# One decoder step on one core: page gathers spread over the first stage, window copies in the last stage, and the first RWKV inversion split with dense products between its parts

## The chip, the cores and the metric

The kernel runs on 1 core of one Trainium2 chip. The metric is the device time of one execution in microseconds (us). The engines of the core are PE (TensorE, with its weight loads shown apart as PEld), DVE (VectorE), ACT (ScalarE), POOL (GpSimd) and SP (SyncE, which here only issues DMAs).

## The reference, cut to what matters

One layer of a hybrid decoder, for a prompt of 512 tokens and for 8 samples of 4 tokens each with a paged cache:

```
x <- x + 1/2 * SwiGLU_1(RMSNorm(x))            # first stage
z  = RMSNorm(x) @ W_in                         # one projection, columns split among the groups
     NSA group:  compressed, selected and window attention branches over paged caches
     RWKV group: token shift, decay, delta-rule state (64 x 64 per head), group norm
x <- x + concat(NSA_out, RWKV_out) @ W_out
x <- x + 1/2 * SwiGLU_2(RMSNorm(x))            # last stage
y  = RMSNorm_final(x)

def cmp_rows(pool, new, pe, w1, w2):           # the samples' compressed keys and values
    past = pool[page_table].reshape(n, PAST_LEN, N_KV_NSA, HEAD_DIM)
    return ... compress(past, pe, w1, w2) ...
def compress(rows, pe, w1, w2):
    blk = rows.reshape(n, length // CMP_BLOCK, CMP_BLOCK, N_KV_NSA, HEAD_DIM) + pe[:, None, :]
    return gelu(einsum('nbcgd,cde->nbge', blk, w1)) @ w2
wb = cache_win_k.shape[1]                      # the window caches, moved on by four rows, are outputs
kw_all = concatenate([cache_win_k, kw], axis=1);  ...  kw_all[:, -wb:], vw_all[:, -wb:]
```

D_MODEL is 1024, D_FF 2816, and all data are fp32. The 8 samples have 16 pages each, 128 pages in all, whose keys and values the first SwiGLU stage gathers and compresses beside its own work.

## The kernel before

The token axis (544 columns: 512 prompt and 32 sample tokens) stays as two halves of 272 columns (HW), and the model axis lies on the partitions. An fp32 product is made of three matmuls on split operands: high part by high part, low by high, high by low (`dense`, L156; `hh`, `hl` are the split activations, `ah`, `al` those of the hidden layer, `wh`, `wl` the split weights). So one 128x128 weight block costs six matmuls of 272 columns.

`wload` (L141) brings a weight tile in chunks of four blocks: SP issues the DMA into `wraw` (L148), ACT copies to `wh` (L150), DVE subtracts to `wl` (L152). Each of the three has three buffers. A chunk feeds 24 matmuls on PE.

`ffn` (L161) is both SwiGLU stages. It runs over 22 hidden tiles `f`, with a gate and an up tile of two chunks each, into PSUM tiles `acc`, and then over 8 output tiles of 22 blocks each. That is 3168 matmuls of 272 columns a stage. In the first stage it calls a hook, `block_step` (L921), before each of the 44 weight tiles of the first part. The hook brings small tables in (f = 1, f = 3), computes the gather indices `idx` (f = 3), issues the copies of the window caches from DRAM to DRAM (f = 14 to 21: two of 254 KB for each f, on SP), and at the steps in `CSTEP` calls `block_pages` (L947).

`block_pages` works on the 128 pages in five groups of 25 or 26 (`CG`). One call multiplies the group that lies in the tile `cp` by the compression weights (64 small matmuls into `hid`, L956), and then gathers the next group into `cp` (`gather`, L915: one indirect DMA on POOL's queue for each page, 128 KB, L918). `cp` has one buffer, so a group's gathers wait for the matmuls of the group before, and then all go out one behind the other.

After the first stage `mix` (L351) does the norm, the input projection (`win_tile`: 48 dense matmuls for each tile) and the RWKV group. `rwkv_prep` (L528) runs twice (`si` 0 and 1), over two head pairs each time, numbered p = 0 to 3 here: it shifts five projected tiles, computes decay and keys, and builds for each chunk of 32 tokens a triangular matrix `L`, with the products of `ar` and `bk` (L598), transposes (L607, L614) and sums (L497, L562, L563). `rwkv_inverse` (L632) inverts all of them for one `si`: DVE transposes `L` into `ivA` (L636, L638), then solves the diagonal 16x16 blocks in a loop of 15 steps of a product and a sum (L653, L654), and transposes the result into `ivDt` and `ivDn` (L656, L658). PE then assembles the off-diagonal blocks in four groups of small matmuls (L664; L672 and L674; L685; L693) with copies on ACT, DVE and POOL between. `rwkv_chain` runs the recurrence.

A scheduler orders the instructions on each engine from their dependences and the order in which the program issues them; those that are passed to `keep_in_program_order` (as `mm` does for a matmul) stay in the order of the program among themselves. In the part around the first inversion the scheduler places the dense matmuls of later projection tiles where PE would wait. Then follow the NSA branches, attention, the output projection and the second `ffn`, which has no hook.

Of the kernel before, what the change touches and what calls it, by code (L numbers as in the profile page):

```python
# [17 lines left out]
KT = 8  # L18
# [8 lines left out]
CSTEP = (8, 15, 22, 29, 36, 43)  # L27
# [21 lines left out]
class Step:  # L49
# [91 lines left out]
    def wload(self, src, n):  # L141
        nc = self.nc
        out = []
        src = src.rearrange("p (k f) -> p k f", f=128)
        for k0 in range(0, n, WK):
            m = min(WK, n - k0)
            w = self.wp.tile([128, WK, 128], F32, name="wraw", tag="wraw", bufs=WB[0])
            nc.sync.dma_start(w[:, :m], src[:, k0:k0 + m])  # L148
            wh = self.wp.tile([128, WK, 128], F32R, name="wh", tag="wh", bufs=WB[1])
            nc.scalar.activation(wh[:, :m], w[:, :m], AF.Copy)  # L150
            wl = self.wp.tile([128, WK, 128], F32R, name="wl", tag="wl", bufs=WB[2])
            nc.vector.tensor_sub(wl[:, :m], w[:, :m], wh[:, :m].bitcast(F32))  # L152
            out += [(wh[:, j], wl[:, j]) for j in range(m)]
        return out
# [184 lines left out]
    def run(self):  # L339
        I, O = self.I, self.O  # L340
        self.setup()
        self.early_w = None
        with ExitStack() as st:
            self.cpool = self.pool("cmp", 1, st)
            self.first_norm()
            self.ffn(I["wg1"], I["wu1"], I["wd1"], I["x"], self.x1, V_MX, self.block_step)
        self.mix()
        self.ffn(I["wg2"], I["wu2"], I["wd2"], self.x2, None, None)
        self.sA.close()

    def mix(self):  # L351
        nc = self.nc
        r = self.norm_end()
        with ExitStack() as st:
# [4 lines left out]
            with ExitStack() as s0:  # L359
                un0 = self.pool("u0", 1, s0, side="right")  # L360
                with ExitStack() as s2:
                    self.rwkv_setup(s2)
                    self.lanes = "p"
                    S0 = self.rwkv_prep(0, r, un0)
                    self.lanes = "q"
                    self.rwkv_inverse(S0[0])
                    self.lanes = "p"
                    S1 = self.rwkv_prep(1, r, un1)
# [4 lines left out]
                self.rwkv_inverse(S1[0])  # L373
# [103 lines left out]

    def shifted(self, i, col, r, tp, xs):
        nc = self.nc
        p = self.win_tile(i)  # L480
# [47 lines left out]
    def rwkv_prep(self, si, r, up):  # L528
# [101 lines left out]
        return L, BK, UV, ar, pcp  # L630

    def rwkv_inverse(self, L):  # L632
        nc, un = self.nc, self.un
        A = un.tile([128, 32, 32], F32, name="ivA", tag="iA")
        Lt = L.rearrange("p x c t -> p t (x c)")
        nc.vector.transpose(A, Lt[:, 0:32])  # L636
        for s in (slice(32, 64), slice(96, 128)):
            nc.vector.transpose(A[s], Lt[s, 32:64])  # L638
# [19 lines left out]
        nc.vector.transpose(Dn.rearrange("p b t -> p t b"), N)  # L658
        grp = [(hh, q, 64 * hh + 32 * q) for q in range(2) for hh in range(2)]
        T = un.tile([128, 16, 16], F32, name="ivT", tag="iN")  # L660
        p = self.ps()
        for c in range(16):
            for hh, q, g in grp:
                nc.tensor.matmul(p[g:g + 32, c * 16:c * 16 + 16], L[g:g + 16, hh, c, 32 * q:32 * q + 32], Dt[g:g + 16, 16 * hh + c, 0:16],  # L664
                                 start=True, stop=True)
        nc.scalar.activation(T, p[:, 0:256].rearrange("p (c s) -> p c s", s=16), AF.Copy, scale=self.half)
# [3 lines left out]
        for c in range(16):  # L670
            for hh, q, g in grp[0:2]:
                nc.tensor.matmul(pt[g:g + 32, c * 16:c * 16 + 16], Dn[g:g + 32, 16 * hh + c], T[g:g + 32, c], start=True, stop=True)  # L672
            for hh, q, g in grp:
                nc.tensor.matmul(pz[g:g + 16, c * 16:c * 16 + 16], T[g:g + 32, c], Dn[g:g + 32, 16 * hh + c, 16:32], start=True, stop=True)  # L674
# [7 lines left out]
        for c in range(16):  # L682
            for hh in range(2):
                g = 64 * hh
                nc.tensor.matmul(p[g + 32:g + 64, c * 32:c * 32 + 32], L[g:g + 32, hh, c, 32:64], Dt[g:g + 32, 16 * hh + c], start=True, stop=True)  # L685
# [4 lines left out]
        for c in range(16):  # L690
            for hh in range(2):
                g = 64 * hh
                nc.tensor.matmul(p[g:g + 32, c * 32:c * 32 + 32], W[g + 32:g + 64, c], L[g + 32:g + 64, hh, c, 32:64], start=True, stop=True)  # L693
        for hh in range(2):
            s = slice(64 * hh, 64 * hh + 32)
            nc.scalar.activation(L[s, hh, :, 32:64], p[s].rearrange("p (c t) -> p c t", t=32), AF.Copy)

# [223 lines left out]
    def block_step(self, step):  # L921
        nc, I, O = self.nc, self.I, self.O
        c = self.cpool
        if step in CSTEP:
            self.block_pages(CSTEP.index(step))
# [3 lines left out]
        if f > 13:  # L929
            n = f - 14  # L930
            for o, x in ((O["owk"][n, :, 0:508], I["wkT"][n, :, 4:512]), (O["owv"][n, 0:508], I["wv"][n, 4:512])):
                self.tc.keep_in_program_order(nc.sync.dma_start(o, x))
        if f == 1:
            self.table_loads()
        if f == 3:
# [9 lines left out]
            nc.vector.tensor_scalar(self.idx, pf[:, 0:128], 128.0, pf[:, 128:129], op0=OP.mult, op1=OP.add)  # L945

    def block_pages(self, at):  # L947
        nc, I, c = self.nc, self.I, self.cpool
        if at > 0:
            i = at - 1  # L950
            k0, m = CG[i], CG[i + 1] - CG[i]
            w = 4 * m + (4 if i == 0 else 0)
            ph = self.ps()
            for j in range(32):
                for x in range(2):
                    nc.tensor.matmul(ph[64 * x:64 * x + 64, 0:w], self.w1[:, x, j], self.cp[:, 0:w // 4, x, j], start=j == 0, stop=j == 31)  # L956
# [675 lines left out]
```

## Time and profile before

| What | Value |
|---|---|
| Runs, us | median 1522.66 of 3, 1521.82 to 1527.6 |
| The profiled execution, us | 1521.93 |
| Its span, us | 1520.1 |
| Mean granted clock of PE | 0.929 of full |
| PE busy | 1367.9 us, 90% of the span, 13337 matmuls |
| DVE, ACT, POOL busy, us | 707.0, 512.1, 250.7 |
| Traffic | 163.25 MB by DMA, mean 107 GB/s |
| Chain that ended last | PE 80%, of which the dense line L159 63%; issue 7%; DVE 6%; ACT 3% |

The profiled execution's own time stands 1.83 us above its span. The page gives shares of the whole span; the stages differ, and they are looked at one by one below. Stretches are named by the time from the span's start: the norm at the first stage's end is at 569.5 us, the RWKV group follows, the output projection starts at 1059.4 us and the last stage right behind it. In a row of a timeline the bracket at the end tells how long the engine was idle before it and what released it; "issue" means that the profile shows nothing that it waited for.

### The profile page before, as it was taken

How to read it: one execution, taken by the hardware profiler on the slowest of the kernel's cores; microseconds unless marked ns; L12 is line 12 of the kernel's file. 1: busy time of each engine (PE TensorE's matmuls, PEld its weight loads, DVE VectorE, ACT ScalarE, POOL GpSimd, SP SyncE). 2: the span in 40 equal slices, each digit the busy share in tenths (PEclk: the TensorE clock that was granted, in tenths of full speed). 3: DMA queues.
4: the chain of work that ended last, by engine and by line, in shares of the span. 5: the costliest groups of instructions: out<-in, count | busy, mean ns of one | idle time of the engine just before them, and what ended most of it. 6: DMA issues, size and time to landing. Idle time of an engine off the chain costs nothing.

```text
span 1520.1 us, 31735 instructions
## 1 busy us (share of the span) xinstructions
PE 1367.9 (90%) x13337; PEld 1272.0 (84%) x13337; DVE 707.0 (47%) x1357; ACT 512.1 (34%) x928; POOL 250.7 (16%) x313
## 2 busy tenths in 40 slices
PE   9969686877799999889899986889999999999996
PEld 8969586766799999778776884567999999999996
DVE  6423222222333345694968764457454444443223
ACT  6212121121232236545222334457443333332321
POOL 2153332415100011212000223320100000000100
PEclk9979697978799999997999997889999999999998
DMA  4533333434334342111131564731532222233332
GB/s 158 186 121 102 94 104 107 139 112 139 94 103 119 114 129 86 43 43 39 37 110 29 171 182 149 215 112 44 175 103 89 87 91 86 89 91 106 109 105 84
DMA packets 99329, 163.25 MB, mean 107 GB/s; under 512 B 16186, under 2 KB 42882, under 8 KB 98547
## 3 DMA queue, kind: packets, MB, share of 16 engines
q1 hardware_dynamic: 74978, 116.10, 25.0%
q0 software_dynamic: 9040, 25.24, 5.6%
q10 hardware_dynamic: 15168, 19.89, 4.4%
q8 instruction: 105, 1.72, 0.5%
q14 instruction: 38, 0.30, 0.1%
HBM read 150.19 MB, written 16.72 MB: 110 GB/s over the span
## 4 chain that ended last, share of the span: by engine, by line
PE 80%; issue 7%; DVE 6%; ACT 3%; another core or an unknown queue 1%; DMA 1%; POOL 0%; ACTq 0%; DVEq 0%; SPq 0%; POOLq 0%
PE acc L159 63%; PE pS L969 1%; PE pq L972 1%; PE po L969 1%; PE pp L969 1%; PE pq L714 1%; PE pq L956 1%; PE pp L956 1%; DMA wraw<-in_wg 1%; PE pp L598 1%; PE pp L796 1%; PE pp L497 1%; PE pp L159 1%; DVE ivt L653 0%
## 5 line engine op out<-in xcount | busy, mean ns | idle before, releaser
L159 PE MATMUL acc<-hl,wh 128*128 128x272 f32 x2064 | 437.9, 296 | 27.5 <-issue 26.4
L150 ACT ACTIVATE wh<-wraw 128x512 fp32r<-128x512 f32 x338 | 209.7, 620 | 685.6 <-PE acc L159 507.1
L159 PE MATMUL acc<-hh,wh 128*128 128x272 f32 x1808 | 394.9, 298 | 33.2 <-issue 29.9
L159 PE MATMUL acc<-hh,wl 128*128 128x272 f32 x1808 | 391.8, 297 | 26.0 <-issue 24.4
L152 DVE TENSOR_TENSOR wl<-wraw,wh 128x512 fp32r<-128x512 f32 x338 | 232.5, 688 | 337.4 <-ACT wh L150 279.7
L159 PEld LDWEIGHTS acc<-hl,wh 128*128 128x128 f32 x2064 | 332.0, 194 | 41.0 <-issue 37.2
L159 PEld LDWEIGHTS acc<-hh,wh 128*128 128x128 f32 x1808 | 296.0, 194 | 42.1 <-issue 35.6
L159 PEld LDWEIGHTS acc<-hh,wl 128*128 128x128 f32 x1808 | 293.2, 194 | 33.5 <-issue 30.5
L918 POOL DMA_INDIRECT cp<-in_cmp,idx x128 | 125.0, 976 | 204.6 <-PE pp L956 80.3
L159 PE MATMUL acc<-ah,wh 128*128 128x272 f32 x660 | 137.0, 289 | 0.0
L159 PE MATMUL acc<-al,wh 128*128 128x272 f32 x660 | 136.2, 287 | 0.0
L159 PE MATMUL acc<-ah,wl 128*128 128x272 f32 x660 | 135.5, 286 | 0.0
L126 POOL TENSOR_TENSOR ss<-ss,sq 128x544 f32<-128x544 f32 x23 | 32.0, 1393 | 599.7 <-ACT sq L122 584.3
L159 PEld LDWEIGHTS acc<-al,wh 128*128 128x128 f32 x660 | 104.0, 188 | 0.0
L159 PEld LDWEIGHTS acc<-ah,wl 128*128 128x128 f32 x660 | 103.3, 188 | 0.0
L159 PEld LDWEIGHTS acc<-ah,wh 128*128 128x128 f32 x660 | 102.9, 188 | 0.0
L194 DVE TENSOR_TENSOR t<-acc,r 128x544 f32<-128x544 f32 x42 | 30.4, 724 | 111.3 <-PE acc L159 87.3
L196 DVE TENSOR_TENSOR u<-acc,r 128x544 f32<-128x544 f32 x42 | 30.4, 724 | 108.8 <-PE acc L159 78.5
L918 POOL DMA_INDIRECT kv<-in_slc,idx x36 | 35.5, 986 | 130.1 <-DVE Y L747 64.2
L199 ACT ACTIVATE ah<-u 128x544 fp32r<-128x544 f32 x44 | 29.0, 658 | 65.1 <-DVE u L197 59.3
L200 DVE TENSOR_TENSOR al<-u,ah 128x544 fp32r<-128x544 f32 x44 | 31.9, 725 | 29.0 <-ACT ah L199 28.3
L1416 ACT ACTIVATE ra<-pq 128x512 f32<-128x512 f32 (+2 forms) x48 | 23.7, 521 | 35.9 <-remote 15.4
(515 smaller groups left out, 1482.0 us busy)
## 6 DMA issues: line engine op xcount, KB each, us to landing
wraw<-in_wg SPq DMA_DIRECT2D x88, 256.0 KB
wraw<-in_wu SPq DMA_DIRECT2D x88, 256.0 KB
wraw<-in_wd SPq DMA_DIRECT2D x80, 256.0 KB
wraw<-in_win SPq DMA_DIRECT2D x50, 256.0 KB
kv<-in_slc SPq DMA_DIRECT2D x60, 128.0 KB
x<-xr ACTq DMA_DIRECT2D x16, 272.0 KB
xr<-x ACTq DMA_DIRECT2D x16, 272.0 KB
wraw<-in_wout SPq DMA_DIRECT2D x16, 256.0 KB
```

What stands on the lines that cost most here:

```text
L126: nc.gpsimd.tensor_add(self.ss, self.ss, sq)
L150: nc.scalar.activation(wh[:, :m], w[:, :m], AF.Copy)
L152: nc.vector.tensor_sub(wl[:, :m], w[:, :m], wh[:, :m].bitcast(F32))
L159: self.nc.tensor.matmul(p[h] if isinstance(p, list) else p[:, h, :HW], a, b[:, h], start=f, stop=l)
L194: nc.vector.tensor_mul(t, pt, r)
L196: nc.vector.tensor_mul(u, pu, r)
L199: nc.scalar.activation(ah[:, f], u, AF.Copy)
L200: nc.vector.tensor_sub(al[:, f], u, ah[:, f].bitcast(F32))
L918: self.nc.gpsimd.indirect_dma_start(out=tile[:, k], out_offset=None, in_=rows, in_offset=bass.IndirectOffsetOnAxis(ap=self.idx[:, k0 + k:k ...
L956: nc.tensor.matmul(ph[64 * x:64 * x + 64, 0:w], self.w1[:, x, j], self.cp[:, 0:w // 4, x, j], start=j == 0, stop=j == 31)
L969: self.tc.keep_in_program_order(self.nc.tensor.matmul(*args, **kw))
L1416: self.nc.scalar.activation(t[:, 0:o + w], p[:, 0:o + w], AF.Copy)
```

## The change

Three things change.

- *Pages.* `block_pages` becomes a generator that stands still between pages. `wload` sends it each converted chunk. For each chunk it may issue 1.25 gathers (`PAGE_RATE`), that is one, and two at every fourth chunk. Ahead of each gather POOL copies one column of the chunk's `wh` into the place in `cp` that the gather will overwrite, so the gather can't go out before ACT has written that `wh`. Three chunks after a group's last page (`PAGE_LAG`) its 64 matmuls are issued. `cp` still has one buffer. The pages begin at f = 3 as soon as `idx` is there and go on through the output tiles.
- *Window copies.* They leave `block_step` and become the hook of the second `ffn`, one copy ahead of each of the weight tiles 4 to 19.
- *Inversion.* `rwkv_inverse` is split. `rwkv_diagonal` makes two full transposes and two copies on ACT in place of one full and two 32-partition transposes, and holds the loop. `rwkv_inverse` keeps its matmuls in program order, and for the first `si` takes 96 dense matmuls of the projection tiles 11 and 12 (`win_ahead`) between its groups: 20, 24, 24 and 28. `rwkv_prep` becomes a generator as well, so that the first inversion is issued behind the first head pair of `si` 1.

What this moves is shown at three places. On POOL in the first stage, `tbl`, `rvd` and `rvr` are tables, `in_cmp` is the page pool and `idx` the page index. Before:

```order
L296 DMA rvr<-rvd 128x3064
L918 DMA cp<-in_cmp,idx 128x256 x128
L469 DMA ident<-in_ident 128x128
L641 MEMSET ivN 128x1024
L642 MEMSET ivN 128x32
```

Now:

```order
L299 DMA rvr<-rvd 128x3064
L1003 COPY cp<-wh 128x1 x5
L957 DMA cp<-in_cmp,idx 128x256 x5
L1003 COPY cp<-wh 128x1 x2
L957 DMA cp<-in_cmp,idx 128x256 x2
L1003 COPY cp<-wh 128x1
L957 DMA cp<-in_cmp,idx 128x256
```

The 128 gathers stood one behind the other; now a copy that reads a chunk's `wh` stands ahead of each one or two of them, down to the last. In the order only the first five are together.

On PE ahead of the first inversion, `xs_wa`, `sq`, `ar` and `bk` belong to head pair 2, and `acc` rows are the dense matmuls. Before:

```order
L562 MATMUL pp<-xs_wa,w2a_5030 128x260
L159 MATMUL acc<-hh,wh 128x272 x2
L159 MATMUL acc<-hl,wh 128x272 x2
L159 MATMUL acc<-hh,wl 128x272
L563 MATMUL pp<-xs_wa,w2a_5030 128x260
L497 MATMUL pp<-sq_6218,blk_5015 128x300
L159 MATMUL acc<-hh,wl 128x272
L497 MATMUL pp<-sq_6218,blk_5015 128x260
L159 MATMUL acc<-hh,wh 128x272 x2
```

Now:

```order
L585 MATMUL pp<-xs_wa,w2a_5142 128x260
L586 MATMUL pp<-xs_wa,w2a_5142 128x260
L520 MATMUL pp<-sq_6086,blk_5127 128x300
L520 MATMUL pp<-sq_6086,blk_5127 128x260
L621 MATMUL pp<-ar,bk_6328 64x128 x2
```

The dense matmuls that stood between these rows, and the 69 that followed the last of them ahead of the inversion, are gone from here; head pair 2's `ar` and `bk` products now come next, and the inversion behind them. Its first group and the dense matmuls that follow:

```order
L637 MATMUL pp<-ident,xs_v 64x64 x16
L520 MATMUL pp<-xs_r,blk_5127 128x300
L520 MATMUL pp<-xs_r,blk_5127 128x260
L1019 MATMUL pq<-ivDt,L 32x16 x64
L1019 MATMUL acc<-hh,wh 128x272 x2
L1019 MATMUL acc<-hl,wh 128x272 x2
```

The tail of head pair 2 (L637, L520) now stands ahead of the inversion; before, its parts lay between the inversion's groups and behind them.

On SP in the last stage, `out_owk` and `out_owv` are the window caches. Now:

```order
L149 DMA wraw<-in_wu 128x512 x2
L987 DMA out_owk<-in_wkT 128x508
L149 DMA wraw<-in_wg 128x512 x2
L987 DMA out_owv<-in_wv 16x4064
L149 DMA wraw<-in_wu 128x512 x2
```

One copy stands between each two weight tiles, where before the copies stood in pairs behind every second one, in the first stage.

The diff, cut to its core:

```diff
...
-CSTEP = (8, 15, 22, 29, 36, 43)
+PAGE_RATE = 1.25
+PAGE_LAG = 3
...
             out += [(wh[:, j], wl[:, j]) for j in range(m)]
+            if self.pages:
+                self.pages.send(wh)
...
-        self.ffn(I["wg2"], I["wu2"], I["wd2"], self.x2, None, None)
+        self.ffn(I["wg2"], I["wu2"], I["wd2"], self.x2, None, None, self.window_copies)
...
-                    S0 = self.rwkv_prep(0, r, un0)
+                    half0 = self.rwkv_prep(0, r, un0)
+                    next(half0)
+                    S0 = next(half0)
...
-                    self.rwkv_inverse(S0[0])
+                    diag = self.rwkv_diagonal(S0[0])
...
-                    S1 = self.rwkv_prep(1, r, un1)
+                    half1 = self.rwkv_prep(1, r, un1)
+                    next(half1)
+                    self.lanes = "q"
+                    self.rwkv_inverse(S0[0], diag, self.win_ahead(11, 12))
+                    self.lanes = "p"
+                    S1 = next(half1)
...
-                self.rwkv_inverse(S1[0])
+                self.rwkv_inverse(S1[0], self.rwkv_diagonal(S1[0]), iter(()))
...
+    def win_ahead(self, *tiles):
+        for i in tiles:
+            wt = self.wload(self.I["win"][i], KT)
+            p = self.made[i] = self.acc()
+            for k in range(KT):
+                xh, xl = self.hh[:, k], self.hl[:, k]
+                for a, b, f, l in ((wt[k][0], xh, k == 0, False), (wt[k][0], xl, False, False), (wt[k][1], xh, False, k == KT - 1)):
+                    for h in range(2):
+                        self.mm(p[:, h, :HW], a, b[:, h], start=f, stop=l)
+                        yield
...
-        p = self.win_tile(i)
+        p = self.made.pop(i) if i in self.made else self.win_tile(i)
...
-        return L, BK, UV, ar, pcp
-    def rwkv_inverse(self, L):
+            yield L, BK, UV, ar, pcp
+    def rwkv_diagonal(self, L):
...
         A = un.tile([128, 32, 32], F32, name="ivA", tag="iA")
...
+        B = un.tile([128, 32, 32], F32, name="ivB", tag="iD")
+        nc.vector.transpose(B, Lt[:, 32:64])
...
         for s in (slice(32, 64), slice(96, 128)):
-            nc.vector.transpose(A[s], Lt[s, 32:64])
+            nc.scalar.activation(A[s], B[s], AF.Copy)
...
+        return Dt, Dn
...
+    def rwkv_inverse(self, L, diag, ahead):
...
+        def fill(n):
+            for _ in range(n):
+                next(ahead, None)
...
-                nc.tensor.matmul(p[g:g + 32, c * 16:c * 16 + 16], L[g:g + 16, hh, c, 32 * q:32 * q + 32], Dt[g:g + 16, 16 * hh + c, 0:16],
+                self.mm(p[g:g + 32, c * 16:c * 16 + 16], L[g:g + 16, hh, c, 32 * q:32 * q + 32], Dt[g:g + 16, 16 * hh + c, 0:16],
...
+        fill(20)
...
+        fill(24)
...
+        fill(24)
...
+        fill(96)
...
-        if step in CSTEP:
-            self.block_pages(CSTEP.index(step))
...
-        if f > 13:
-            n = f - 14
-            for o, x in ((O["owk"][n, :, 0:508], I["wkT"][n, :, 4:512]), (O["owv"][n, 0:508], I["wv"][n, 4:512])):
-                self.tc.keep_in_program_order(nc.sync.dma_start(o, x))
...
-    def block_pages(self, at):
+            self.pages = self.block_pages()
+            next(self.pages)
+    def window_copies(self, step):
+        nc, I, O = self.nc, self.I, self.O
+        n, odd = divmod(step - 4, 2)
+        if 0 <= n < 8:
+            o, x = (O["owv"][n, 0:508], I["wv"][n, 4:512]) if odd else (O["owk"][n, :, 0:508], I["wkT"][n, :, 4:512])
+            self.tc.keep_in_program_order(nc.sync.dma_start(o, x))
+    def block_pages(self):
...
-        if at > 0:
-            i = at - 1
+        due, wh = 0.0, (yield)
+        for i in range(len(CG) - 1):
...
+            cp = c.tile([128, 26, 2, 32, 4], F32, name="cp")
+            cf = cp.rearrange("p k x j c -> p k (x j c)")
+            if i == 0:
+                nc.sync.dma_start(cf[:, m], I["cpe"])
+            for k in range(m):
+                while due < 1.0:
+                    wh = yield
+                    due += PAGE_RATE
+                due -= 1.0
+                nc.gpsimd.tensor_copy(cf[:, k, 0:1], wh[:, 0, 0:1].bitcast(F32))
+                self.gather(cf[:, k:k + 1], I["cmp"], k0 + k, 1)
+            for _ in range(PAGE_LAG):
+                yield
...
-                    nc.tensor.matmul(ph[64 * x:64 * x + 64, 0:w], self.w1[:, x, j], self.cp[:, 0:w // 4, x, j], start=j == 0, stop=j == 31)
+                    nc.tensor.matmul(ph[64 * x:64 * x + 64, 0:w], self.w1[:, x, j], cp[:, 0:w // 4, x, j], start=j == 0, stop=j == 31)
...
-        if at < 5:
-            k0, m = CG[at], CG[at + 1] - CG[at]
-            self.cp = c.tile([128, 26, 2, 32, 4], F32, name="cp")
-            cf = self.cp.rearrange("p k x j c -> p k (x j c)")
-            if at == 0:
-                nc.sync.dma_start(cf[:, m], I["cpe"])
-            self.gather(cf, I["cmp"], k0, m)
+        self.pages = None
+        yield
...
```

More of the change, by code (lines that the diff above doesn't have):

```diff
@@ L341, in run @@
         self.setup()
-        self.early_w = None
+        self.early_w = self.pages = None
         with ExitStack() as st:
@@ L346, in run @@
             self.ffn(I["wg1"], I["wu1"], I["wd1"], I["x"], self.x1, V_MX, self.block_step)
+            assert self.pages is None
         self.mix()
-        self.ffn(I["wg2"], I["wu2"], I["wd2"], self.x2, None, None)
+        self.ffn(I["wg2"], I["wu2"], I["wd2"], self.x2, None, None, self.window_copies)
         self.sA.close()
@@ L353, in mix @@
         r = self.norm_end()
+        self.made = {}
         with ExitStack() as st:
@@ L658, in rwkv_inverse @@
         nc.vector.transpose(Dn.rearrange("p b t -> p t b"), N)
+        return Dt, Dn
+    def rwkv_inverse(self, L, diag, ahead):
+        nc, un = self.nc, self.un
+        Dt, Dn = diag
+        def fill(n):
+            for _ in range(n):
+                next(ahead, None)
         grp = [(hh, q, 64 * hh + 32 * q) for q in range(2) for hh in range(2)]
@@ L671, in rwkv_inverse @@
             for hh, q, g in grp[0:2]:
-                nc.tensor.matmul(pt[g:g + 32, c * 16:c * 16 + 16], Dn[g:g + 32, 16 * hh + c], T[g:g + 32, c], start=True, stop=True)
+                self.mm(pt[g:g + 32, c * 16:c * 16 + 16], Dn[g:g + 32, 16 * hh + c], T[g:g + 32, c], start=True, stop=True)
             for hh, q, g in grp:
-                nc.tensor.matmul(pz[g:g + 16, c * 16:c * 16 + 16], T[g:g + 32, c], Dn[g:g + 32, 16 * hh + c, 16:32], start=True, stop=True)
+                self.mm(pz[g:g + 16, c * 16:c * 16 + 16], T[g:g + 32, c], Dn[g:g + 32, 16 * hh + c, 16:32], start=True, stop=True)
+        fill(24)
         for hh, q, g in grp[0:2]:
@@ L684, in rwkv_inverse @@
                 g = 64 * hh
-                nc.tensor.matmul(p[g + 32:g + 64, c * 32:c * 32 + 32], L[g:g + 32, hh, c, 32:64], Dt[g:g + 32, 16 * hh + c], start=True, stop=True)
+                self.mm(p[g + 32:g + 64, c * 32:c * 32 + 32], L[g:g + 32, hh, c, 32:64], Dt[g:g + 32, 16 * hh + c], start=True, stop=True)
+        fill(24)
         for hh in range(2):
@@ L692, in rwkv_inverse @@
                 g = 64 * hh
-                nc.tensor.matmul(p[g:g + 32, c * 32:c * 32 + 32], W[g + 32:g + 64, c], L[g + 32:g + 64, hh, c, 32:64], start=True, stop=True)
+                self.mm(p[g:g + 32, c * 32:c * 32 + 32], W[g + 32:g + 64, c], L[g + 32:g + 64, hh, c, 32:64], start=True, stop=True)
         for hh in range(2):
```

## The prediction

> **What bounds the kernel now.** I read the profile page first, then busy time by stretches of the first stage, then the waits there, then the timelines of PE and POOL through one gather burst. On the page, two rows of the span in 40 slices (38 us each):
>
> ```profile
> PE   9969686877799999889899986889999999999996
> PEclk9979697978799999997999997889999999999998
> ```
>
> PE (TensorE matmul) is at 90% or more nearly everywhere except in slices 3 to 11, the first stage. Its granted clock falls in the same slices. The busy time of each engine in stretches of that stage (stretch; length; then PE, PEld, DVE, ACT, POOL as busy time and instruction count; granted clock; DMA share; GB/s):
>
> ```profile
> 83.00:105.60 22.60, 10.76 (x36) 7.66 (x36) 3.38 (x5) 1.92 (x3) 15.27 (x16) 0.62 0.39 119
> 105.60:147.00 41.40, 41.39 (x399) 41.09 (x398) 15.85 (x25) 10.91 (x17) 8.54 (x9) 0.96 0.31 94
> 147.00:172.60 25.60, 8.70 (x28) 5.70 (x26) 0.69 (x1) 0.63 (x1) 16.52 (x18) 0.62 0.37 106
> 172.60:219.80 47.20, 47.11 (x438) 46.74 (x439) 17.80 (x27) 12.73 (x20) 8.72 (x9) 0.95 0.31 95
> 219.80:245.20 25.40, 7.13 (x24) 5.09 (x23) 0.69 (x1) 0.63 (x1) 16.27 (x17) 0.60 0.36 105
> 245.20:293.00 47.80, 47.74 (x446) 47.25 (x446) 19.06 (x29) 12.73 (x20) 9.12 (x10) 0.96 0.43 127
> 293.00:317.80 24.80, 7.90 (x26) 5.54 (x24) 0.69 (x1) 0.63 (x1) 15.96 (x17) 0.57 0.35 106
> 317.80:364.60 46.80, 46.75 (x431) 46.48 (x432) 17.80 (x27) 12.72 (x20) 7.92 (x9) 0.94 0.43 130
> 364.60:389.50 24.90, 7.24 (x27) 5.24 (x25) 0.69 (x1) 0.63 (x1) 15.95 (x17) 0.57 0.40 121
> 389.50:426.50 37.00, 36.97 (x355) 36.70 (x356) 15.43 (x24) 10.80 (x17) 0.00 (x0) 0.92 0.35 101
> ```
>
> Five stretches of 22.6 to 25.6 us hold 24 to 36 matmuls each; between them PE is full. In all five POOL is busy with 16 to 18 instructions, and DVE and ACT do nearly nothing. What POOL does there, and how PE moves at the start and the end of the second one:
>
> ```profile
> 136.02 0.94 POOL L918 DMA_INDIRECT cp<-in_cmp,idx  x1 [33.18 <-PE pq L956]
> 137.27 0.95 POOL L918 DMA_INDIRECT cp<-in_cmp,idx  x1 [0.30 <-issue]
> ...
> 167.75 0.95 POOL L918 DMA_INDIRECT cp<-in_cmp,idx  x1 [0.30 <-issue]
> ```
>
> ```profile
> 147.75 0.41 PE L159 MATMUL acc<-hl,wh 128*128 128x272 f32 x2
> 148.82 0.41 PE L159 MATMUL acc<-hh,wl 128*128 128x272 f32 x2 [0.66 <-issue]
> ...
> 171.97 0.38 PE L159 MATMUL acc<-hh,wh 128*128 128x272 f32 x1 [1.02 <-issue]
> 172.68 0.81 PE L159 MATMUL acc<-hl,wh 128*128 128x272 f32 x2 [0.33 <-issue]
> ```
>
> The burst is 26 gathers, one each 1.25 us, from 136.02 to 167.75. PE runs at full rate for the first 11 us of it, then issues a pair of matmuls in a us or more, until 4.9 us after the last gather has started. The waits over the stage (waiting line and its releaser; us in total, times, longest):
>
> ```profile
> ACT wh L150 <- PE acc L159: 116.6, 39, 21.2
> PE acc L159 <- issue: 80.7, 79, 2.4
> POOL cp L918 <- PE pp L956: 80.3, 2, 40.4
> ```
>
> ACT waits for PE (for a free weight buffer), not PE for ACT; PE waits for nothing that the profile names. DMA is at 35 to 40% in the stalls and at 43% in two stretches where PE is full, so bandwidth isn't it. A run of gathers takes something that PE's issue needs. The trace doesn't show what it is.
>
> **Term 1, the stalls.** The steady rate is that of the last stage, the same kind of dense work without gathers:
>
> ```profile
> 1125.00:1480.00 355.00, 355.00 (x2837) 355.00 (x2837) 145.24 (x217) 113.62 (x178) 6.83 (x5) 1.00 0.31 94
> ```
>
> 355.00 / 2837 = 0.1251 us a matmul. The five stalls last 22.6 + 25.6 + 25.4 + 24.8 + 24.9 = 123.3 us and hold 141 matmuls, worth 141 x 0.1251 = 17.6 us. Lost: 105.7 us. After each, PE is full but on a lower clock: 41.4 x 0.04 + 47.2 x 0.05 + 47.8 x 0.04 + 46.8 x 0.06 + 37.0 x 0.08 = 11.7 us. Together 117.4 us, the most that pacing can give back.
>
> **Does pacing give it back?** A weight chunk feeds 24 matmuls, 24 x 0.1251 = 3.00 us. At 1.25 gathers a chunk there is one gather each 2.40 us, in pairs every fourth chunk. Whatever gathers occupy, in the burst it was free 36.7 us after the first of 26 (136.02 to 172.68), which is at most 1.41 us each. At 2.40 us no backlog can form. Nearest rows for a short run and a longer one are in the attention stage (POOL's gathers, then PE):
>
> ```profile
> 962.52 0.94 POOL L918 DMA_INDIRECT kv<-in_slc,idx  x1 [4.24 <-PE pp L969]
> ...
> 968.77 0.94 POOL L918 DMA_INDIRECT kv<-in_slc,idx  x1 [0.30 <-issue]
> ...
> 1015.80 0.94 POOL L918 DMA_INDIRECT kv<-in_slc,idx  x1 [7.45 <-PE pp L969]
> ...
> 1018.30 0.95 POOL L918 DMA_INDIRECT kv<-in_slc,idx  x1 [0.31 <-issue]
> ```
>
> ```profile
> 961.00:974.00 13.00, 10.34 (x93) 7.46 (x91) 4.56 (x17) 4.37 (x13) 5.67 (x6) 0.81 0.70 193
> ```
>
> ```profile
> 1019.16 0.63 PE L972 MATMUL pp<-ident,S 128*128 128x128 f32 x4 [0.29 <-issue]
> ```
>
> Six in a row cost PE 13.00 - 10.34 = 2.66 us, 0.44 a gather; three in a row 0.29 us, 0.10 a gather. Single gathers and pairs lie below that. The bounds for what stays are 0 and 128 x 0.10 = 12.4 us. I take 4, a third of it, since the first eight of a burst leave no gap at all.
>
> The other costs of the paging are hidden. Each gather gets a 128x1 copy on POOL that reads the chunk's wh. The nearest row:
>
> ```profile
> L489 POOL COPY sho<-zp 128x1 f32<-128x1 f32 x14 | 4.0, 287 | 0.0
> ```
>
> So POOL needs 0.95 + 0.30 + 0.29 = 1.5 us per 2.40, and nothing on PE's path is queued behind a copy that waits for ACT: the norm's partial sums (L126) are used only after the stage. wh's three buffers now also wait for POOL; the copy comes at the chunk's start, PE reads it for 3 us, so PE is last. The next group's first copy waits for the 64 block matmuls that free cp. They stand three chunks (9 us) after the group's last gather, so they find it landed. If that lag were too short, PE would wait one landing a group, a few us over five groups; that lies inside my range. The last block matmuls stand 132 dense ones, 16.5 us, before the stage's end.
>
> **Term 2, the window copies: 0.** The same 16 transfers, one per weight tile, move on SP from the end of the first stage to the last one. The rows 245.20:293.00 and 317.80:364.60 had them, at 127 and 130 GB/s, with PE full (47.74 of 47.80, 46.75 of 46.80). The last stage moves 94 GB/s without them. What hides them is the slack of the weight loads; without it, each would cost its own time, 0.26 MB at 94 GB/s, 16 x 2.8 = 44 us.
>
> **Term 3, the first inversion.** The stretch before the inversion, the inversion with the second half's tail, and the dense matmuls (L159) alone in the first of them:
>
> ```profile
> 656.00:680.50 24.50, 20.57 (x131) 18.09 (x129) 23.60 (x49) 12.84 (x19) 1.85 (x10) 0.93 0.14 42
> 680.50:708.60 28.10, 25.15 (x669) 22.22 (x669) 14.89 (x26) 10.13 (x20) 9.13 (x13) 0.70 0.11 33
> 708.60:786.00 77.40, 71.91 (x1106) 62.34 (x1105) 60.49 (x108) 25.64 (x40) 4.05 (x10) 0.98 0.25 79
> ```
>
> ```profile
> 656.00:680.50 24.50, 17.74 (x117) 0.93 0.14 42
> ```
>
> In the first, DVE is full (23.60 of 24.50: the diagonal's loop), and 117 dense matmuls run beside it at no cost. The change takes 96 of them, tiles 11 and 12, out of there and puts them between the inversion's products, behind the tail of preparation 2. DVE's chain stays, so PE now idles beside it, and 96 x 0.1251 = 12.0 us of PE work come after it. What they can fill there is PE's idle time in the second row, 28.10 - 25.15 = 2.95 us. So +9.0 us; the third row (PE 71.91 of 77.40) leaves little to take it up. Bounds: +17, if nothing is filled and the 96 run at the clock of that row (12.0 / 0.70); -3, if PE's later idle time takes up all 12 and the gaps are filled.
>
> The diagonal's transposes and the nearest ACT copy:
>
> ```profile
> L638 DVE STREAM_TRANSPOSE ivA<-L 32x1024 f32<-32x1024 f32 x2 | 4.0, 2008 | 0.0
> L636 DVE STREAM_TRANSPOSE ivA<-L 128x1024 f32<-128x1024 f32 x1 | 2.0, 1979 | 0.0
> L688 ACT ACTIVATE ivW<-pq 32x512 f32<-32x512 f32 x4 | 2.4, 588 | 5.2 <-PE pq L685 5.1
> ```
>
> DVE goes from 1.98 + 2 x 2.01 = 6.0 us to 2 x 1.98 = 4.0, but two ACT copies of twice the ACT row's length (about 1.0 us each, an estimate from it) follow before the loop can start. Per inversion -2 to 0; I take 0.
>
> **Sum.** From the profiled execution's 1521.93 us (0.7 below the median of the runs, 1522.66): - 105.7 - 11.7 + 4 + 0 + 9.0 = 1417.5. I predict 1417 us. Its own bounds: 1521.93 - 117.4 - 3 - 4 = 1397.5 with nothing left of the stalls, and 1521.93 - 117.4 + 12.4 + 17 = 1434.
>
> **Rivals.** *A, paced gathers still cost.* If each costs what one of six in a row did, 0.44 us, 56 us stay: 1521.93 - 117.4 + 56 + 9 = 1470. Against it: eight gathers pass without a gap, and three cost 0.29 us. 0.09.
>
> *B, slower: a gather blocks PE's issue for as long as it is served, whenever it comes.* Bursts hid part of that, since PE ran 11 us into each on what it held already; a pace of one per chunk hides nothing if that store isn't refilled. Place: all the stage from the first page on; price up to 1.41 us a gather, 128 x 1.41 = 180 us: 1521.93 - 117.4 + 180 + 9 = 1594. It decides against the change from (117.4 - 9) / 128 = 0.85 us a gather. Against it: the gap after three gathers. 0.04.
>
> *C, the change doesn't do what it says: POOL runs behind and gathers bunch again.* Then the stalls stay and term 3 is added, 1521.93 + 9 = 1531. Against it: a copy needs a converted chunk, and with three wh buffers four gathers at most can be let go at once. 0.04.
>
> *D, POOL and DVE in turn.* The burst at 136.02 ran while DVE was nearly idle; now descriptors are made beside its subtractions. The first gather of all, beside DVE at work, took longer:
>
> ```profile
> 69.58 1.50 POOL L918 DMA_INDIRECT cp<-in_cmp,idx  x1 [13.70 <-DVE u L196]
> ```
>
> If the two exclude each other, a gather's 1.50 + 0.29 us and DVE's share of a full stretch (15.43 of 37.00, 0.42 x 2.40 = 1.0 us) need 2.8 us where there are 2.40: 17% of 128 x 2.40 = 307 us, 51 us more, 1468. With the 0.95 us of most rows the sum is 2.2 us and PE stays the bound. 0.04.
> The Trainium skill, SBUF — State Buffer, in its table of who interferes with whom, speaks for D: DVE and GpSimd share a port pair as an exclusive lock, held for a whole instruction, and descriptors made on GpSimd wait for it. By that rule alone the sum would be D's if every gather met it, and 15 us above the forecast's if one in two did; the 1.50 us row may show it, most rows of the bursts can't, because DVE stood still there.
>
> **How the numbers follow.** The forecast has 0.79, A 0.09, B 0.04, C 0.04, D 0.04. A and D at half their price reach 1445 and 1443; the range 1398 to 1445 takes the forecast's bounds and those halves and leaves A and D in full, B and C out, under 2 in 10. About 0.5% (7.6 us) is what a measurement of this kernel can tell from no change. Faster by more: forecast, A and D, 0.92. Slower: B and half of C, whose 1531 lies at the line, 0.06. Same: 0.02.
>
> **What would show it.** Right: in the changed profile no stretch of the first stage with PE under 90%, clock 1.0 there, single gathers 2.4 us apart, PE's wait for issue near zero; the last stage still at 0.125 us a matmul at some 135 GB/s; PE with a gap of about 12 us beside the diagonal's loop. Wrong: issue gaps of PE at each gather (A or B, told apart by their length), gathers 1.25 us apart in runs over six (C), subtractions of DVE over 0.7 us and PE waiting for wl (D), PE waiting for weights in the last stage (term 2).

## The result, and the profile after

The changed kernel takes 1422.72 us (median of 4 runs, 1418.88 to 1427.67), the kernel before 1523.03 us (median of 4): ratio 0.9338, 95% interval 0.9301 to 0.9375. The forecast was 1417 us, between 1398 and 1445. The profiled execution took 1418.88 us with a span of 1417.1, 103.0 us less than the span before.

The two rows of the page that showed the first stage's holes before:

```profile
PE   8999999999999995899999777899999999999996
PEclk9999999999999996799899978899999999999998
```

From the second slice to the end of the first stage (slice 13 now, 35 us each) none lies under 9, in busy time or in clock; the first, the start-up, is much as before. The same by stretches, and the last stage in the last row:

```profile
60.00:140.00 80.00, 78.12 (x696) 76.98 (x696) 32.91 (x52) 22.76 (x36) 37.35 (x57) 1.00 0.51 160
140.00:220.00 80.00, 80.00 (x720) 79.72 (x719) 32.83 (x50) 23.10 (x36) 41.68 (x56) 1.00 0.41 124
220.00:300.00 80.00, 80.00 (x720) 79.72 (x719) 34.01 (x51) 24.40 (x38) 37.38 (x55) 1.00 0.42 129
300.00:380.00 80.00, 80.00 (x719) 79.72 (x718) 26.63 (x38) 21.71 (x36) 45.85 (x62) 1.00 0.54 157
380.00:453.00 73.00, 73.00 (x664) 72.57 (x662) 25.37 (x42) 22.57 (x37) 31.07 (x42) 1.00 0.49 145
...
1022.00:1377.00 355.00, 355.00 (x2838) 355.00 (x2837) 145.56 (x217) 113.62 (x178) 6.84 (x5) 1.00 0.35 105
```

PE is full and its clock is whole, while POOL is at work for half of every stretch. The only 1.9 us that PE lacks lie in the first stretch. The last stage has its 2838 matmuls in 355.00 us, as before, with the window copies in it (105 GB/s over the stage, 94 before). All that PE waited for in the stage, as the waits list it from 60 to 453 us:

```profile
PE acc L162 <- issue: 1.7, 4, 0.8
```

Before, it was 80.7 us in 79 waits. POOL between 139 and 150 us, a pair and then single gathers:

```profile
139.50 0.82 POOL L1003 COPY cp<-wh 128x1 f32<-128x1 f32 x2 [1.33 <-ACT wh L151]
140.48 0.97 POOL L957 DMA_INDIRECT cp<-in_cmp,idx  x1 [0.15 <-POOL cp L1003]
141.75 0.95 POOL L957 DMA_INDIRECT cp<-in_cmp,idx  x1 [0.30 <-issue]
142.71 0.67 POOL L1003 COPY cp<-wh 128x1 f32<-128x1 f32 x1
143.65 0.98 POOL L957 DMA_INDIRECT cp<-in_cmp,idx  x1 [0.27 <-POOL cp L1003]
145.51 0.71 POOL L1003 COPY cp<-wh 128x1 f32<-128x1 f32 x1 [0.88 <-ACT wh L151]
146.49 0.97 POOL L957 DMA_INDIRECT cp<-in_cmp,idx  x1 [0.27 <-POOL cp L1003]
148.61 0.18 POOL L1003 COPY cp<-wh 128x1 f32<-128x1 f32 x1 [1.15 <-ACT wh L151]
149.06 1.14 POOL L957 DMA_INDIRECT cp<-in_cmp,idx  x1 [0.27 <-POOL cp L1003]
```

The copies that POOL was idle for are released by ACT's wh, so the gathers follow the weights. The norm row of PE marks the ends of the stages, first of the kernel before, then of the changed one:

```profile
569.50 0.73 PE L135 MATMUL pp<-ss,ones 128*128 128x272 f32 x2
...
1119.79 0.62 PE L135 MATMUL pp<-ss,ones 128*128 128x272 f32 x2
```

```profile
453.18 0.73 PE L136 MATMUL pp<-ss,ones 128*128 128x272 f32 x2
...
1017.12 0.62 PE L136 MATMUL pp<-ss,ones 128*128 128x272 f32 x2
```

| Part, us | Before | After | Change |
|---|---|---|---|
| First stage, to its norm row | 569.50 | 453.18 | -116.3 |
| Between the two norm rows | 550.3 | 563.9 | +13.6 |
| From the second norm row to the end of the span | 400.3 | 400.0 | -0.3 |

The middle part lost where the inversion was. PE beside the diagonal's loop and behind it, in the timeline and by stretches:

```profile
552.04 2.22 PE L520 MATMUL pp<-sq,blk 128*128 128x300 f32 x4
568.97 1.98 PE L621 MATMUL pp<-ar,bk 64*64 64x128 f32 x32 [14.71 <-DVE ar L614]
```

```profile
552.00:569.00 17.00, 2.29 (x9) 1.18 (x8) 16.83 (x25) 6.80 (x9) 1.30 (x7) 0.50 0.01 3
569.00:607.00 38.00, 35.71 (x756) 32.45 (x756) 11.69 (x22) 12.04 (x22) 5.14 (x13) 0.82 0.11 35
```

PE stands still for 14.71 us until DVE, full at 16.83 of 17.00, comes to `ar`. Then it works off the tail, the inversion and the 96 dense matmuls one after the other.

### The profile page after: what moved, and what is told of

It reads as the page before. It is cut to its first block, busy times and chain, and to the rows that moved or that the text cites. A ratio compares the mean times of both kernels' runs of the same rounds, so it can differ in the third digit from the quotient of the medians.

```text
span 1417.1 us, 32001 instructions
## 1 busy us (share of the span) xinstructions
PE 1329.6 (94%) x13337; PEld 1249.2 (88%) x13337; DVE 703.8 (50%) x1355; ACT 518.3 (37%) x933; POOL 304.4 (21%) x441
## 3 DMA queue, kind: packets, MB, share of 16 engines
q0 software_dynamic: 9040, 25.24, 6.1%
## 4 chain that ended last, share of the span: by engine, by line
PE 83%; DVE 8%; ACT 3%; issue 2%; DMA 1%; another core or an unknown queue 1%; POOL 0%; ACTq 0%; SPq 0%; DVEq 0%; POOLq 0%
PE acc L162 65%; PE po L1019 2%; PE pq L1022 1%; PE pS L1019 1%; PE pq L1011 1%; PE pp L1019 1%; PE acc L1019 1%; PE pq L753 1%; PE pp L621 1%; PE pq L1019 1%; PE pp L1011 1%; DVE ivt L678 1%; PE pp L520 1%; PE pp L162 1%
## 5 line engine op out<-in xcount | busy, mean ns | idle before, releaser
L162 PE MATMUL acc<-hl,wh 128*128 128x272 f32 x2032 | 417.2, 291 | 1.4 <-ACT on L1481 0.7
L162 PE MATMUL acc<-hh,wl 128*128 128x272 f32 x1776 | 374.1, 291 | 4.2 <-DVE wl L153 3.3
L162 PE MATMUL acc<-hh,wh 128*128 128x272 f32 x1776 | 376.4, 292 | 1.7 <-ACT hh L110 0.7
L162 PEld LDWEIGHTS acc<-hl,wh 128*128 128x128 f32 x2032 | 317.8, 189 | 6.3 <-issue 3.3
L162 PEld LDWEIGHTS acc<-hh,wh 128*128 128x128 f32 x1776 | 282.2, 190 | 7.0 <-issue 2.9
L162 PEld LDWEIGHTS acc<-hh,wl 128*128 128x128 f32 x1776 | 280.2, 190 | 6.3 <-DVE wl L153 3.8
L957 POOL DMA_INDIRECT cp<-in_cmp,idx x128 | 129.4, 1011 | 42.5 <-POOL cp L1003 25.8
L1003 POOL COPY cp<-wh 128x1 f32<-128x1 f32 x128 | 52.6, 423 | 118.7 <-ACT wh L151 62.5
```

Of the source, the lines that this page charges most:

```text
L162: self.nc.tensor.matmul(p[h] if isinstance(p, list) else p[:, h, :HW], a, b[:, h], start=f, stop=l)
L957: self.nc.gpsimd.indirect_dma_start(out=tile[:, k], out_offset=None, in_=rows, in_offset=bass.IndirectOffsetOnAxis(ap=self.idx[:, k0 + k:k ...
L1003: nc.gpsimd.tensor_copy(cf[:, k, 0:1], wh[:, 0, 0:1].bitcast(F32))
```

## The experiments

Each kernel was timed beside the kernel before on the same chip. Beside the first four below that one took 1522.61 us (median of 7); beside `no_tie`, the two with runs and the plain DMAs 1531.15 us (one run, as those are); beside `diag_only`, `free_order` and the two faster paces (these one run each) 1531.47 us (median of 9). The latter eight therefore stand some 0.6% above what the expectations count from. The part between the norm rows varies: eight kernels that have it word for word as the changed kernel took 563.9, 566.6, 568.6, 568.9, 572.2, 574.2, 576.4 and 578.4 us for it. That of the changed kernel's profile is the least of the eight. A few us are not read from single profiles there.

### What gave the gain and what gave back: parts alone

*Paging and window copies alone* (`pages_copies`). The edit undoes the inversion's split:

```diff
-                    self.rwkv_inverse(S0[0], diag, self.win_ahead(11, 12))
+                    self.rwkv_inverse(S0[0])
```

> The paging and the moved window copies alone; the inversion and its preparation as before. Theory: the changed kernel gained 116.3 us by the end of the first stage and gave 13.3 back behind it, all of it because 96 dense matmuls no longer run beside the diagonal's loop. Then this kernel runs 12 to 15 us faster than the changed one, at 1408 to 1411 us by the medians. Rival: what was given back comes from the last stage with the window copies in it, or from a general slowing behind a denser first stage. Then this kernel stays at 1418 to 1425 us.

Measured: 1407.80 us, ratio 0.9245 (0.9226 to 0.9264); the part between the norm rows 552.7 us. As the theory had it (0.2 us below its range). The last stage with the copies in it isn't the cause of the loss: it has them here too and the loss is gone.

*No dense products in the inversion* (`no_fill`):

```diff
-                    self.rwkv_inverse(S0[0], diag, self.win_ahead(11, 12))
+                    self.rwkv_inverse(S0[0], diag, iter(()))
```

> The whole change, but the first inversion gets no dense matmuls between its groups; tiles 11 and 12 are made in the ordinary place, where the scheduler may put them. Theory: the scheduler puts them beside the diagonal's loop again and the 16.8 us in which PE stood still there are filled: 1409 to 1414 us. Rival: the loss lies in the inversion's own order (all its matmuls in program order, behind the whole tail of head pair 2) and in the ACT copies of the diagonal. Then it stays within 3 us of the changed kernel, 1420 to 1426 us.

Measured: 1415.36 us, ratio 0.9297 (0.9279 to 0.9316), between the theory and its rival. The dense matmuls did go back beside the loop, but not all of the time came back. By the profiles, head pair 3 starts (its first matmul with `w2a`) 153.9 us behind the norm row in the changed kernel, 144.1 here and 140.3 with paging and copies alone (139.1 in the kernel before). So 9.8 us go with the dense products and about 4 to 5 with something else. (The eight profiles of the same code have 151.6 to 156.4 us for the first of these marks, so the 9.8 stands for some 8 to 12; by the medians the dense products cost 7.4.) The two runs below look for that.

*The inversion's split alone* (`inverse_only`): the kernel before with only the inversion's part of the diff.

> The kernel before with the split inversion alone; gathers in five bursts, copies in the first stage. Theory: the first stage is as before and the loss behind it is the same 13 to 15 us: 1535 to 1539 us. Rival: the loss needs the full first stage ahead of it (a clock or buffer state that it leaves behind). Then it stays near 1523 us.

Measured: 1542.49 us, ratio 1.0140 (1.0119 to 1.0161), 20 us slower and 3.5 above the theory's range. The split is a loss by itself, with the five stalls still ahead of it; the full first stage isn't needed. Its profile shows PE's idle time at the same place, 14.96 us until `ar`.

*Window copies back in the first stage* (`copies_back`):

```diff
+        if f > 13:
+            n = f - 14
+            for o, x in ((O["owk"][n, :, 0:508], I["wkT"][n, :, 4:512]), (O["owv"][n, 0:508], I["wv"][n, 4:512])):
+                self.tc.keep_in_program_order(nc.sync.dma_start(o, x))
```

> The whole change, but the window copies stay in the first stage, two for each f from 14 on, beside the paced gathers. Theory: they cost nothing in either place, so the time is that of the changed kernel within 4 us, 1419 to 1427 us, and PE is full in the first stage. Rival: paced gathers and copies together hold up weights in the first stage, by up to their own 44 us, 1430 to 1467 us.

Measured: 1427.62 us, ratio 0.9367 (0.9342 to 0.9392), against 0.9338 (0.9301 to 0.9375) for the changed kernel. The intervals overlap; the median is 0.6 us above the theory's range and below the rival's. The copies go out from 183 to 274 us here. In the stretch that holds most of them PE is full, at 161 GB/s (129 in the changed kernel):

```profile
220.00:300.00 80.00, 80.00 (x720) 79.72 (x719) 34.07 (x51) 23.88 (x38) 38.39 (x55) 1.00 0.53 161
```

The first stage ends at 456.3 us, beside 453.2 to 456.2 us in the five kernels with the same paging and the copies moved. So the copies hold nothing up there, and moving them was worth nothing that these runs can tell.

*The diagonal's transposes alone* (`diag_only`), on top of paging and copies, the inversion in one piece:

```diff
-        for s in (slice(32, 64), slice(96, 128)):
-            nc.vector.transpose(A[s], Lt[s, 32:64])
+        B = un.tile([128, 32, 32], F32, name="ivB", tag="iD")
+        nc.vector.transpose(B, Lt[:, 32:64])
...
+        for s in (slice(32, 64), slice(96, 128)):
+            nc.scalar.activation(A[s], B[s], AF.Copy)
```

> Paged gathers and moved window copies, the inversion in one piece in its old place and order, with only the diagonal's transposes changed (two full ones and two ACT copies). Theory: DVE saves 2 us and ACT's copies add 2 us on the chain; the time is that of the paging and copies alone, 1405 to 1411 us. Rival: the ACT copies stand behind ACT's other work and cost 3 us or more for each inversion: 1413 to 1416 us, which would explain what the change without dense products still lost.

Measured: 1414.92 us beside 1531.47, ratio 0.9245 (0.9218 to 0.9271), the ratio of paging and copies alone. No cost and no gain that these runs can tell.

*The order of the inversion left free* (`free_order`), without dense products (the edit, of which one place is shown, holds for both inversions):

```diff
-                self.mm(p[g:g + 32, c * 16:c * 16 + 16], ...
+                nc.tensor.matmul(p[g:g + 32, c * 16:c * 16 + 16], ...
```

> The whole change without dense products between the groups, and with the inversion's matmuls left to the scheduler. Theory: the 7.6 us that the change without dense products still lost to the paging and copies alone come from the fixed order, which puts the inversion behind the whole tail of head pair 2; with the order free the time is 1406 to 1410 us. Rival: they come from the later place of the inversion in the program or the diagonal's ACT copies; then it stays at 1413 to 1418 us.

Measured: 1410.63 us beside 1531.47, ratio 0.9214 (0.9187 to 0.9241), below the 0.9297 (0.9279 to 0.9316) with the order fixed, clear of its interval. PE's first wait behind the dense matmuls, first with the order fixed and then free:

```profile
PE pp L621 <- DVE ar L614: 10.8, 3, 7.2
```

```profile
PE pq L699 <- DVE ivDt L681: 3.8, 1, 3.8
```

With the order fixed, PE waits 7.2 us for `ar` of head pair 2 before it may begin the inversion. Left free, it begins with the inversion as soon as `ivDt` is there, 3.8 us after its last dense matmul, and takes head pair 2's tail between the groups. Head pair 3 then starts 139.0 us behind the norm row, as in the kernel before (139.1). So the rest of the loss is the fixed order, and it is lost at the first inversion.

### What in the bursts starves PE

*No POOL copy ahead of the gathers* (`no_tie`): the change without what paces it.

```diff
-                nc.gpsimd.tensor_copy(cf[:, k, 0:1], wh[:, 0, 0:1].bitcast(F32))
```

> The whole change without the POOL copy ahead of each gather, so nothing holds a gather back but its group's free tile. Theory: it is the pace alone that gives the gain; without it the gathers run 1.25 us apart again, PE is starved in five stretches, and 100 to 117 us come back: 1520 to 1540 us. Rival: the place of the block matmuls and the window copies in the last stage gave a part of the gain; then it stays clearly under 1520.

Measured: 1546.90 us beside 1531.15. The first stage ends at 576.1 us, with all five stalls:

```profile
PE acc L162 <- issue: 84.9, 83, 3.1
```

The time is above the range; with 0.6% taken off for that chip it is 1538 us, inside it. The stalls are all back. The copy is what the gain hangs on.

*Runs of eight and of thirteen at the same mean pace* (`bunch8`, `bunch13`), one POOL copy ahead of each run (8 or 13 in place of N):

```diff
+                if k % N == 0:
+                    while due < min(N, m - k):
+                        wh = yield
+                        due += PAGE_RATE
```

> The whole change at the same mean pace, but gathers let go in bunches of eight, one POOL copy ahead of each bunch. Theory: PE has some 11 us in hand at the start of a run of gathers and is starved from then until 5 us after the last one has started; eight take 7 x 1.25 = 8.8 us, so a bunch starves PE for 0 to 2.6 us, 17 bunches, 1420 to 1465 us. Rival: only the mean pace counts, whatever the bunches; then 1419 to 1427. Second rival: each gather in a row costs PE 0.44 us, as in the run of six in the attention stage; then 128 x 0.44 = 56 us more, about 1479.

> As the bunches of eight, with bunches of 12 and 13, two a group. Theory: 12 x 1.25 + 5 - 11 = 9 us of starving in each of ten bunches, of which PE still does a seventh, and some 2 us of half clock behind each: 95 us more, about 1517. If only the mean pace counts: 1419 to 1427. If each gather in a row costs 0.44: about 1479, the same as the bunches of eight.

Measured: 1447.13 and 1520.84 us beside 1531.15, the first inside the theory's range, the second near its 1517 (1512 with 0.6% taken off). The cost of a run by its length, as dense matmuls in a stretch from its first gather to 8 us behind the last one's start. A run of 5 and one of 8 (kernel of eights), one of 13 (kernel of thirteens), and a burst of 26 (kernel before):

```profile
412.56:425.96 13.40, 13.40 (x109) 1.00 0.67 206
236.72:254.07 17.35, 16.83 (x135) 1.00 0.48 143
```

```profile
178.53:202.55 24.02, 20.50 (x135) 0.86 0.42 127
```

```profile
136.02:175.75 39.73, 22.75 (x129) 0.72 0.37 108
```

At 0.1251 us a matmul they lost 0 (13.40 - 109 x 0.1251 = -0.2), 0.5, 7.1 and 23.6 us. From 13 to 26 gathers that is 16.5 us for 13, 1.27 us each: their own spacing of 1.25 us. Little is lost up to about eight; beyond that, nearly all of the time is. Counted in the same way, two more runs of eight lost 0.1 and 0.9 us, two more of 13 7.2 and 7.1. The first stage of the kernel of eights ends at 471.2 us, 18.0 later than with the even pace: 0.14 us for each of 128 gathers. A price of 0.44 us a gather, or a mean pace that alone counts, would give neither row.

The kernel of thirteens lost 87 us in its first stage, not only by starving: behind the second run of three groups, by the waits, the block matmuls come before the pages have landed.

```profile
PE pp L1013 <- DMA cp<-in_cmp,idx: 16.7, 2, 9.7
PE pq L1013 <- DMA cp<-in_cmp,idx: 8.1, 1, 8.1
```

A run of 13 lasts 16 us, and the lag is three chunks, 9 us. So its total agrees with the theory in part by a cost that the theory didn't have; the 7.1 us of a group's first run, against 7.7 expected (six sevenths of 9), is the clean number.

*Plain DMAs in the same bursts* (`plain_dma`): the kernel before, each indirect gather replaced by a DMA of 128 KB from POOL's queue.

```diff
-            self.nc.gpsimd.indirect_dma_start(out=tile[:, k], ...
+                self.nc.gpsimd.dma_start(tile[:, k], rows[128 * (k0 + k):128 * (k0 + k) + 128])
```

> The kernel before, with each indirect gather of the first stage replaced by a plain DMA of the same 128 KB from POOL's queue, page after page in the pool (the pages that the table names are not looked up, so the compressed keys and values are those of other pages). Theory: it is not the bytes that starve PE but what an indirect gather does on its way; then PE stays full and the first stage ends as in the changed kernel, 1400 to 1415 us. Rival: the bytes, or any DMA issued from POOL in a long run, starve PE; then the five stretches stay, 1490 to 1525 us.

Measured: 1406.56 us beside 1531.15. The first stage ends at 451.9 us with no pacing at all. A burst on POOL, and PE in the stretch around it:

```profile
164.88 10.59 POOL L919 DMA_DIRECT2D cp<-in_cmp  x20 [34.09 <-PE pp L959]
```

```profile
140.00:220.00 80.00, 80.00 (x800) 79.45 (x799) 30.53 (x47) 21.87 (x34) 20.77 (x40) 1.00 0.49 153
```

Twenty DMAs of the same bytes go out in 10.59 us, more than twice as dense, and PE loses nothing. The profile's list of DMA queues has 9040 packets and 25.24 MB on q0, software_dynamic, in this run as in the kernel before, so the packets are as many and as large. So it is neither bytes nor packets nor a run of DMAs from POOL, but the indirect form.

One more suspect can be looked up in the trace of the kernel before: the loading of PE's own instructions, since PE waits there for "issue" alone. Queue q8 brings instructions in 105 packets of 16 KB, one for some 254 of the 26,674 instructions on PE and PEld, so these are taken to be PE's. Packets start at 142.63 and at 183.19 us, and none between. PE is starved from 147 to 172 us, and then runs at full rate for 10 us on what had been brought in ahead of the stall. So its instructions were there.

*Faster paces* (`pace171`, `pace150`), in pairs:

```diff
-PAGE_RATE = 1.25
+PAGE_RATE = 1.75
```

> The whole change with gathers in pairs, one POOL copy a pair, at 1.75 a weight chunk: one gather each 1.71 us on average. The bunches of 8, 13 and 26 left their last gather's start 2.3, 3.0 and 4.9 us before PE ran free, which fits a queue that serves one gather in 1.40 us while they come each 1.25 us (1.40 + 0.15 for each one before). Theory of that queue: at 1.71 us it empties behind each pair, PE isn't starved and the time is that of the changed kernel, 1417 to 1428 us. Rival: what PE lacks is a share of something that each gather takes for longer than 1.40 us; then PE shows waits on issue in a group's later gathers and the time is over 1435 us.

> As the last, at 2.0 a chunk: a pair each 3.00 us, one gather each 1.50 us. Theory of the queue: it still empties, for 0.2 us behind each pair. If PE only needs it to be empty now and then, the time stays at 1417 to 1428 us; if PE needs it free for as long as it takes to bring in its next instructions (a seventh of full rate came through in the stalls), PE is slowed from 11 us into each group of 38 us, and the time is 1440 to 1500 us. POOL itself is near full, 2 x 1.25 + 0.42 of 3.00 us.

Measured: 1437.00 and 1444.39 us beside 1531.47, above the theory's range, the first by no more than a single run can tell when 0.6% are taken off for the chip (1429 and 1436). The first stage ends at 463.0 and 473.7 us, 9.8 and 20.5 later than in the changed kernel. But most of the loss is not spread. In the kernel of 1.50 us, the first group and then the stretch of the later ones:

```profile
69.40:100.40 31.00, 21.43 (x130) 0.81 0.47 138
...
150.00:230.00 80.00, 80.00 (x743) 1.00 0.47 144
```

At the start 18 gathers go out in a row, since the chunks run ahead while `idx` is not there yet; that run costs 31.00 - 130 x 0.1251 = 14.7 us. Behind it, in the second row, PE is full at one gather per 1.50 us within the groups; from 230 to 350 us its waits for issue come to 3.0 us. This fits a queue that PE only needs to be empty now and then (no row shows the queue itself), and the rival of a longer share falls; where I missed was the first run's length.

## Why the prediction was right, point by point

**Right: the stalls go with the pace.** The first stage gave back 116.3 us of the 117.4 that were there. I had left 4 us of stalls; 1 was left. Rival A's 0.44 us a gather did not come: spread gathers cost nothing, and runs of eight 0.14 us a gather. Rival B's is the opposite of what the runs of 5 and 8 show. C's condition is `no_tie`, and its stalls are all back there; with the copies the gathers held their distance. D asked for DVE's subtractions over 0.7 us and PE waiting for wl. In the stage they take 709 ns on average (692 before), so the first sign is there; a gather takes 1.011 us (0.976 before), and PE's list of waits has no wl.

What D supposes does happen, and costs little. DVE beside the POOL rows shown above:

```profile
139.47 0.69 DVE L153 TENSOR_TENSOR wl<-wraw,wh 128x512 fp32r<-128x512 f32 x1
142.66 0.68 DVE L153 TENSOR_TENSOR wl<-wraw,wh 128x512 fp32r<-128x512 f32 x1
145.48 0.69 DVE L153 TENSOR_TENSOR wl<-wraw,wh 128x512 fp32r<-128x512 f32 x1 [2.14 <-ACT wh L151]
148.67 0.68 DVE L153 TENSOR_TENSOR wl<-wraw,wh 128x512 fp32r<-128x512 f32 x1
```

POOL's copy and DVE's subtraction wait for the same `wh`. The copies at 142.71 and 145.51 us start 0.05 and 0.03 us behind a subtraction and end 0.04 and 0.05 us behind its end; the one at 148.61 starts ahead of it and takes 0.18 us. The gather at 149.06 starts inside a subtraction and takes 1.14 us. Of the 128 copies 54 take over 0.6 us and 63 under 0.2; 15 of the 128 gathers take over 1.1 us, 13 before. The Trainium skill (SBUF — State Buffer, Who interferes with whom) has a VectorE instruction with two SBUF inputs contend with a GpSimd instruction that reads SBUF, for ports that are an exclusive lock; the prediction had left out this condition. The trace agrees for the copies, which read `wh`. The same section has tensor_tensor not stalling a DMA; these gathers, which read `idx`, do wait for one. These waits cost PE nothing, because POOL has time left (its share below is 1.7 us of 2.40); on average a gather is 0.035 us longer than before.

**Right: the copies cost nothing.** The last stage keeps its 0.1251 us a matmul, at 129 GB/s from 1022 to 1110 us, where the copies go out (I had put some 135).

**Right in kind, too small: term 3.** I had +9.0 us (12.0 less 2.95 of gaps), with bounds of -3 and +17. The profiled execution shows +13.6; by medians the split costs 14.9 us on top of paging and copies (1422.72 against 1407.80) and 19.9 alone, the latter beyond my bound. The step that failed is the sum's "what they can fill there", which priced only the dense matmuls. Those cost about what I had put down, 9.8 us by the start of head pair 3. What I gave no price is the fixed order: the inversion waits behind the tail of head pair 2, which itself waits for DVE. I had named the place (behind the tail of preparation 2) and not the wait.

**A size that hid.** POOL's copy takes 0.42 us on average, not 0.29, for the reason under D; POOL's share is 1.7 us of 2.40, and stays covered. Under C I had four gathers at most let go at once; the first twelve go out nearly in a row, within 16 us, since chunks had run ahead while `idx` was not there, and cost the 1.9 us that PE lacks in the first stretch.

For the profiled execution the sum then reads 1521.93 - 116.3 + 13.6 - 0.3 = 1418.9. My two misses there, 2.9 us too little gained and 4.6 us too little lost, nearly cancel; that the total comes within 2 us of 1417 is luck, and this execution is the fastest of the four. In the five other kernels with this paging the first stage ends at 454.9 to 456.3 us, so the gain is 113 to 116 us and my 113.4 lies in it. What is left is term 3, too small by 6 to 11 us by the medians, and the median of 1422.72 lies above the forecast by 5.7.

## What to carry to other kernels

When an engine is starved while nothing in the profile holds it, look for what another engine does in a row at that time, and lay the run's length against the loss: the slope (here the run's own spacing) and the start (here some eight gathers) tell more than the mean. A run of indirect gathers is cheapest spread over dense work by a real dependence on that work; here one gather each 1.50 us still did, in steady run. A fixed order with filling work between its parts pays only if that work had no better place; here it had run for nothing beside a loop on DVE, and the best versions tried are those that left it there (ratios 0.9245 and 0.9214, against 0.9338).

## What the runs showed of the hardware

- Indirect gathers from POOL, 1.25 us apart, leave PE at full rate for about 11 us (some eight gathers) beside these dense matmuls and then let 24 to 36 matmuls through in 23 to 26 us, a fifth to a ninth of full rate by this count, until a few us after the last one has started. In the attention stage a run of six already cost 2.66 us. The same bytes by plain DMAs from POOL, 0.53 us apart, don't touch PE.
- What is shared isn't settled. It is not bandwidth (35 to 40% DMA share in the stalls), not the weights, not the number of DMAs or of their packets, and not the loading of PE's instructions (none was loaded from 143 to 183 us, and PE ran on at full rate from 172.7). Whether it lies in the reading of the index or in how the descriptors are made was not tried.
- In steady run a gather each 1.50 us, in pairs, leaves PE full (80.00 of 80.00 us).
- A 128x1 copy on POOL that starts within a DVE subtraction of two SBUF tiles waits for its end: it takes up to 0.71 us, and 0.17 to 0.20 else. An indirect gather that starts within one takes up to 1.5 us in place of 0.97.
